# GpSimd's and ScalarE's part in the last block of a projection kernel: own weights, earlier copies, and partial dot products added in PSUM

## The chip, the cores and the metric

One core of a Trainium2 chip runs the whole program. The metric is the device time of one execution in microseconds; the kernel before took 636.08 us (median of 3 runs, 635.98 to 636.09).

Names used below: PE is the matrix engine (PEld its weight loads), DVE is VectorE, ACT is ScalarE, POOL is GpSimd, SP issues the loads. In the profile's lines CUSTOM_DVE_ANT_0 is DVE's dot product, TENSOR_TENSOR on POOL its product, ACTIVATE on ACT the sum of that product, and TENSOR_TENSOR_SCAN a scan. "A.", "V.", "G.", "T." and "SY." in code are ACT, DVE, POOL, PE and SP.

## The reference

```python
def setup_inputs():
    B, S, D = 8, 2048, 4096
    return {"x": randn(B, S, D), "w": randn(D, 1)}        # float32

def reference(x, w):
    proj = (x @ w).squeeze(-1)
    cm = np.maximum.accumulate(proj, axis=1)
    is_record = (proj >= cm).astype(np.float32)
    return np.cumsum(is_record, axis=1).astype(np.float32)
```

x has 268 MB, and every element is used once. The work is a dot product of length 4096 for each of 8 x 2048 positions, then a running maximum and a running count along 2048.

## The kernel before

Positions 0 to 1919 are handled in five groups of 384 (three rows of 4096 for each of 128 partitions), positions 1920 to 2047 in a tail of 128 (one row for each partition and batch row). Each dot product is split by columns. DVE multiplies and sums the first columns, with w in PSUM (`w_v`). POOL multiplies the others, with w in SBUF, and ACT sums POOL's products. PE brings the sums of all 128 partitions into 8 rows of PSUM by a matmul with the identity. DVE then runs three short instructions there: the maximum scan, the comparison, and the count scan.

```python
CM = 3072; CP = 2688; CL = 2304      # DVE's columns: in the groups, tiles 0-2, tiles 3-5
PIECES = {                           # the last two batch rows in pieces (start, split, end)
    1: [(1280, 3072, D), (0, 768, 1280)],
    0: [(2816, 3584, D), (1792, 2432, 2816), (1024, 1536, 1792),
        (512, 1024, 1024), (0, 512, 512)],
}
# ...
def scans(cm_, cnt_, n, cm0, cnt0):
    V.tensor_tensor_scan(out=cm_, data0=ps[:, :n], data1=neg[:, :n], ...)    # running max
    V.tensor_tensor(out=rec[:, :n], in0=ps[:, :n], in1=cm_, op=ALU.is_ge)
    V.tensor_tensor_scan(out=cnt_, data0=rec[:, :n], data1=rec[:, :n], initial=cnt0,
                         op0=ALU.add, op1=ALU.max)                           # running count
# ... ACT's loop over the groups ends with
            A.wait_ge(at, 1)         # DVE's queue raises at once it has gone past its scans
# ... the tail
A.copy(out=w_sb[:, CP:], in_=w_p)._wait_ge(fr[NS - 2], 2 * NK // NS).then_inc(wc, 1)
A.copy(out=w_sb[:, :CP], in_=w_v[:, :CP])._wait_ge(ge, NG).then_inc(wc, 1)
V.wait_ge(wc, 3)                     # both copies
G.wait_ge(wc, 2)                     # the first copy
for m, b in enumerate(last):         # six whole tiles, batch rows 7 to 2
    # ... DVE: columns below VC, PSUM w; POOL: the others, w_sb; ACT: sum of POOL's
for i, (b, (c0, v, c1)) in enumerate(tails):          # seven pieces, batch rows 1 and 0
    # ... DVE's dot is seeded with the sum of the piece before, so it waits for that one
lhs = [sum_p] + parts + [sum_v]      # POOL's sums of the pieces, then DVE's one sum
for k, l in enumerate(lhs):
    i = T.matmul(out=ps[:, :P], lhsT=l, rhs=identity, start=k == 0, ...)._wait_ge(*waits[k])
scans(cm_l, cnt_l, P, ...)
```

`w_sb` is a copy of all of w in an x buffer that has come free; `w_p` holds columns 2688 to 4095 of w in SBUF from the start. A copy is needed for POOL's other columns: the Trainium skill ("PSUM — Partial Sum Buffer", Specifications (TRN2)) has GpSimd neither read nor write PSUM.

## Time and profile before

| | before |
|---|---|
| time | 636.08 us |
| span in the profile | 634.0 us |
| mean load rate | 424 GB/s |
| last load lands | 623.44 us |
| last POOL product ends | 628.5 us |
| first short scan of the tail starts | 630.15 us |

Two rows of the profile's page, 40 equal slices of the span with busy tenths:

```profile
POOL 0444555544444444555444444555544444445496
DMA  9999999999999999999999999999999999999992
```

Loads fill the span until the last slice. POOL is at 4 or 5 tenths in the groups and still in slice 38, and full in slice 39. So only the end can be changed without moving fewer bytes.

When the last load landed is read from the issues of the last load's line (engine, operation, duration in ns, start; then time to landing). It was issued at 598.5 and landed 24.9 us later, at 623.44 with one more digit:

```profile
L191 SPq DMA_DIRECT2D xbuf<-in_x_dram x1: 4214/4214/4214, 598.5 to 598.5; - x1
DMA to landing us min/median/max: 24.9/24.9/24.9
```

The timeline of the end (start us, duration us, engine, line, operation, out<-in, shapes, count, and the idle time before with what ended it):

```profile
584.59 6.69 POOL L250 TENSOR_TENSOR xbuf<-xbuf,w_p 128x3072 f32<-128x3072 f32 x1 [7.81 <-POOLq L251]
...
598.98 1.01 DVE L139 TENSOR_TENSOR_SCAN cnt<-rec,cnt 8x384 f32<-8x384 f32 x1
599.26 1.36 ACT L285 COPY xbuf<-w_p 128x1408 f32<-128x1408 f32 x1 [4.72 <-ACTq L267]
600.53 2.39 ACT L286 COPY xbuf<-w_v 128x2688 f32<-128x2688 f32 x1
600.77 21.30 POOL L296 TENSOR_TENSOR xbuf<-xbuf 128x1408 f32<-128x1408 f32 x6 [9.49 <-ACT xbuf L285]
...
603.07 2.95 DVE L125 CUSTOM_DVE_ANT_0 xbuf<-xbuf,w_v 128x2688 f32<-128x2688 f32 x1 [3.09 <-ACT xbuf L286]
...
622.01 6.48 POOL L321 TENSOR_TENSOR xbuf<-xbuf 128x1024 f32<-128x1024 f32 x5
...
630.15 0.47 DVE L132 TENSOR_TENSOR_SCAN cm_l<-ps,cm,neg 8x128 f32<-8x128 f32 x1 [3.22 <-PE ps L336]
```

POOL's last group product ended at 584.59 + 6.69 = 591.28. POOL then stood idle for 9.49 us until ACT's first copy, although the first tail tile had landed at 589.20. ACT had been held back by its wait for DVE's scans (`at`). (DVE's queue raises such a signal when it has gone past the scans, not when they are done: ACT began 0.28 us after the count scan's start, and before its end at 599.99.) From 600.77 on POOL's eleven products run back to back for 27.7 us, and the chain of waits (start, duration, what) is nothing but them until ACT and PE finish:

```profile
599.26 1.37 ACT xbuf L285
...
603.89 18.19 POOL xbuf L296 x5
622.08 5.74 POOL xbuf L321 x4
...
628.51 1.61 PE ps L336 x6
```

### The profile page before, as it was taken

To read this page: it belongs to the slowest core of one execution; us is meant where nothing else is said; L and a number is where in the kernel's file an instruction comes from. 1 tells how busy PE (TensorE), PEld (TensorE's weight loads), DVE (VectorE), ACT (ScalarE), POOL (GpSimd) and SP (SyncE) were. 2 spreads that over 40 slices of the span, in tenths; PEclk is the share of its full clock that TensorE was granted. 3 is DMA by queue.
4 is the path that set the end of the run, shared out by engine and by line. 5 is a ranking of instruction groups with operands and counts; after the bars stand their busy time and mean duration, and the time that the engine had idled before them with its cause. 6 is when DMAs were issued, how large, how long until landed. Compare 5 with 4: busy or idle time off the path is not lost. (4 is left out here: it accounts for less than half of the span.)

```text
span 634.0 us, 1167 instructions
## 1 busy us (share of the span) xinstructions
PE 29.8 (5%) x84; PEld 13.1 (2%) x84; DVE 434.0 (68%) x286; ACT 149.0 (24%) x267; POOL 296.7 (47%) x59
## 2 busy tenths in 40 slices
PE   8000000010000001000000100000001000000101
PEld 3000000000000000000000000000000000000000
DVE  0666777787666678777776676777778766667695
ACT  1222222223222222222222222222222322222344
POOL 0444555544444444555444444555544444445496
DMA  9999999999999999999999999999999999999992
GB/s 389 409 443 440 440 409 443 441 432 422 443 437 432 425 443 437 431 425 440 440 423 434 437 443 416 440 437 441 419 440 434 443 412 447 435 444 407 431 424 110
DMA packets 7746, 268.54 MB, mean 424 GB/s; under 512 B 904, under 2 KB 952, under 8 KB 1728
## 3 DMA queue, kind: packets, MB, share of 16 engines
q1 hardware_dynamic: 7728, 268.50, 98.1%
q10 hardware_dynamic: 16, 0.02, 0.0%
q14 instruction: 2, 0.02, 0.0%
HBM read 268.45 MB, written 0.07 MB: 424 GB/s over the span
## 5 line engine op out<-in xcount | busy, mean ns | idle before, releaser
L125 DVE CUSTOM_DVE_ANT_0 xbuf<-xbuf,w_v 128x3072 f32<-128x3072 f32 (+3 forms) x128 | 415.1, 3293 | 176.6 <-DMA xbuf<-in_x_dram 173.6
L250 POOL TENSOR_TENSOR xbuf<-xbuf,w_p 128x3072 f32<-128x3072 f32 x40 | 267.7, 6693 | 321.5 <-POOLq L251 321.5
L257 ACT ACTIVATE xbuf<-xbuf 128x1024 f32<-128x1024 f32 x120 | 125.4, 1046 | 455.9 <-POOL xbuf L250 455.9
L273 PE MATMUL ps<-identity,small 128*8 128x128 f32 x60 | 13.6, 418 | 566.6 <-ACT xbuf L257 566.6
L296 POOL TENSOR_TENSOR xbuf<-xbuf 128x1408 f32<-128x1408 f32 (+1 forms) x6 | 21.3, 3598 | 9.5 <-ACT xbuf L285 9.5
L257 ACT ACTIVATION_READ_ACCUMULATOR xbuf<-xbuf 128x1 f32 x120 | 22.4, 187 | 0.0
L273 PEld LDWEIGHTS ps<-identity,small 128*8 128x8 f32 x60 | 7.3, 129 | 574.0 <-ACT xbuf L257 570.1
L132 DVE TENSOR_TENSOR_SCAN cm<-ps,cm,neg 8x384 f32<-8x384 f32 x5 | 5.0, 1004 | 15.3 <-PE ps L273 15.3
L145 PE MATMUL w_v<-w_row,identity 8*128 8x512 f32 x14 | 12.1, 1056 | 0.0
L300 ACT ACTIVATE xbuf<-xbuf 128x1408 f32<-128x1408 f32 (+1 forms) x6 | 9.2, 1537 | 11.2 <-POOL xbuf L296 11.2
L125 DVE DVE_READ_ACCUMULATOR2_ANT small<- 128x1 f32 x133 | 11.0, 82 | 0.0
L321 POOL TENSOR_TENSOR xbuf<-xbuf 128x512 f32<-128x512 f32 (+3 forms) x5 | 6.5, 1342 | 0.0
L139 DVE TENSOR_TENSOR_SCAN cnt<-rec,cnt 8x384 f32<-8x384 f32 x5 | 5.0, 1007 | 0.2
L145 PEld LDWEIGHTS w_v<-w_row,identity 8*128 8x128 f32 x14 | 4.6, 332 | 7.3 <-issue 7.3
L125 DVE CUSTOM_DVE_ANT_0 xbuf<-xbuf,w_v,small 128x512 f32<-128x512 f32 (+2 forms) x5 | 4.1, 827 | 0.7
L336 PE MATMUL ps<-identity,small 128*8 128x128 f32 x8 | 2.2, 406 | 30.6 <-ACT xbuf L326 30.6
L326 ACT ACTIVATE xbuf<-xbuf 128x512 f32<-128x512 f32 (+3 forms) x5 | 3.3, 651 | 1.4 <-POOL xbuf L321 1.3
L136 DVE TENSOR_TENSOR rec<-ps,cm 8x384 f32<-8x384 f32 x5 | 2.7, 546 | 0.2
L132 DVE TENSOR_TENSOR_SCAN cm_l<-ps,cm,neg 8x128 f32<-8x128 f32 x1 | 0.5, 471 | 3.2 <-PE ps L336 3.2
L285 ACT COPY xbuf<-w_p 128x1408 f32<-128x1408 f32 x1 | 1.4, 1365 | 4.7 <-ACTq L267 4.7
L286 ACT COPY xbuf<-w_v 128x2688 f32<-128x2688 f32 x1 | 2.4, 2392 | 0.0
L145 PE MATMUL ps<-w_row,identity 8*128 8x512 f32 x2 | 2.1, 1136 | 3.1 <-DMA w_row<-in_w_dram 3.1
(19 smaller groups left out, 8.9 us busy)
## 6 DMA issues: line engine op xcount, KB each, us to landing
xbuf<-in_x_dram SPq DMA_DIRECT2D x40, 6144.0 KB, 47.8
xbuf<-in_x_dram SPq DMA_DIRECT2D x6, 2048.0 KB, 42.7
xbuf<-in_x_dram SPq DMA_DIRECT2D x1, 1408.0 KB, 36.8
xbuf<-in_x_dram SPq DMA_DIRECT2D x2, 640.0 KB, 38.5
xbuf<-in_x_dram SPq DMA_DIRECT2D x1, 512.0 KB, 39.8
xbuf<-in_x_dram SPq DMA_DIRECT2D x2, 256.0 KB, 26.8
xbuf<-in_x_dram SPq DMA_DIRECT2D x1, 384.0 KB, 32.2
out_dram<-cnt SPq DMA_DIRECT2D x5, 12.0 KB
```

Source lines behind the costliest of these rows:

```text
L125: return V.tensor_tensor_reduce(out=xsl, in0=xsl, in1=wsl, scale=1.0, scalar=seed, op0=ALU.mult, op1=ALU.add, accum_out=dst,)
L132: V.tensor_tensor_scan(out=cm_, data0=ps[:, :n], data1=neg[:, :n], initial=cm0, op0=ALU.max, op1=ALU.max,)._wait_ge(psr, 1).then_inc(psr, 1)
L136: V.tensor_tensor(out=rec[:, :n], in0=ps[:, :n], in1=cm_, op=ALU.is_ge)._wait_ge(psr, 2).then_inc(psr, 1)
L139: V.tensor_tensor_scan(out=cnt_, data0=rec[:, :n], data1=rec[:, :n], initial=cnt0, op0=ALU.add, op1=ALU.max,)._wait_ge(psr, 3).then_inc(cs, 1)
L145: return T.matmul(out=w_v[:n, k * WC : (k + 1) * WC] if k < CV // WC else ps_w, lhsT=identity[:NW, k : k + 1].to_broadcast([NW, n]), rhs=w ...
L250: G.tensor_mul(out=xm, in0=xm, in1=w_m)._wait_ge(xg, 1).then_inc(pg, 1)
L257: i = A.activation(out=xr, in_=xr, func=ACTF.Copy, accum_out=sums_p[:, j * B + b : j * B + b + 1],)
L273: i = T.matmul(out=ps[:, j:NP:R], lhsT=l[:, j * B : (j + 1) * B], rhs=identity, start=l is sums_p, stop=l is sums,)
L296: G.tensor_mul(out=xb[:, VC:D], in0=xb[:, VC:D], in1=w_sb[:, VC:D])._wait_ge(xt[m], 16).then_inc(pl, 1)
L300: A.activation(out=xb[:, VC:D], in_=xb[:, VC:D], func=ACTF.Copy, accum_out=sum_p[:, b : b + 1],)._wait_ge(pl, npool)
L321: G.tensor_mul(out=xl, in0=xl, in1=w_sb[:, v:c1])._wait_ge(xq[i], 16).then_inc(pl, 1)
L326: A.activation(out=xl, in_=xl, func=ACTF.Copy, accum_out=pacc[:, b : b + 1])._wait_ge(pl, npool).then_inc(pa, 1)
```

## The change

The intent is to start the tail earlier and to take waits out of it. (1) POOL's first three tail tiles read `w_p`, which is there from the start. (2) ACT no longer waits for the last group's scans, and PE gives its signal `ge` once DVE's and ACT's sums are there, so both copies of w run beside PE and the scans. (3) In the tail every DVE dot product starts from zero instead of the sum before it (it is no longer "seeded"); PE adds all sums of a batch row in PSUM, nine of them instead of four. The trace shows two matmul records (passes) for each sum, called a pair below. 320 columns of the last pieces go from DVE to POOL.

```diff
-            (1024, 1536, 1792),
-            (512, 1024, 1024),
+            (1024, 1408, 1792),
+            (512, 832, 1024),
 ...
+        A.sem_inc(at, 1)
         with A.Fori(0, NG):
+            A.wait_ge(at, 1)
+            A.sem_inc(at, -1)
 ...
-            A.wait_ge(at, 1)
-            A.sem_inc(at, -1)
         with T.Fori(0, NG):
             T.wait_ge(ga, 1)
-            T.wait_ge(gd, 1)
-            for j in range(R):
-                for l in (sums_p, sums):
+            T.sem_inc(ga, -1)
+            for l in (sums_p, sums):
+                if l is sums:
+                    T.wait_ge(gd, 1)
+                    T.sem_inc(ge, 1)
+                for j in range(R):
                     i = T.matmul(
                         out=ps[:, j:NP:R], lhsT=l[:, j * B : (j + 1) * B],
-                        rhs=identity, start=l is sums_p, stop=l is sums,
+                        rhs=identity, start=l is sums_p and j == 0,
+                        stop=l is sums and j == R - 1,
                     )
 ...
-        V.wait_ge(wc, 3)
+        V.wait_ge(wc, 2)
 ...  # in the tail, one helper for whole tiles and pieces
+            dot(xb[:, c0:v], w_v[:, c0:v], sum_v[piece][:, b : b + 1])._wait_ge(arrived, 16)...
+            if v < c1:
+                wb = w_p[:, v - CP : c1 - CP] if npool < R else w_sb[:, v:c1]
+                if npool == R:
+                    G.wait_ge(wc, 2)
 ...  # PE's order: for each piece of batch row 0, DVE's sum and then POOL's
+                order.append((sum_v[piece], sd, len(last) + i + 1))
+                if v < c1:
+                    order.append((sum_p[piece], pa, npool))
```

With `start` now set on the first of six matmuls alone, the others find columns not yet written in this round. The Trainium skill ("PSUM — Partial Sum Buffer", The four PSUM rules) says that a starting matmul clears the written-marks of its whole 2 KiB bank (in the groups of 32 partitions that it writes), and that a later matmul overwrites where the mark is clear.

More of the change, by code (lines that the diff above doesn't have):

```diff
@@ L64 @@
     }
-    NPART = max(sum(v < c1 for _, v, c1 in p) for p in PIECES.values()) - 1
+    NPART = max(len(p) for p in PIECES.values())
     pool = ctx.enter_context(tc.tile_pool(name="sb", bufs=1))
@@ L98 @@
     sums_p = cut(R * B)
-    sum_v = cut(B)
-    sum_p = cut(B)
-    parts = [cut(B) for _ in range(NPART)]
     tails = [(b, p) for b in sorted(PIECES, reverse=True) for p in PIECES[b]]
-    acc = cut(len(tails))
+    sum_v = [cut(B) for _ in range(NPART)]
+    sum_p = [cut(B) for _ in range(NPART)]
     def row(k):
@@ L122, with dot @@
     V, A, G, T, SY = nc.vector, nc.scalar, nc.gpsimd, nc.tensor, nc.sync
-    def dot(xsl, wsl, seed, dst):
+    def dot(xsl, wsl, dst):
         return V.tensor_tensor_reduce(
-            out=xsl, in0=xsl, in1=wsl, scale=1.0, scalar=seed,
+            out=xsl, in0=xsl, in1=wsl, scale=1.0, scalar=0.0,
             op0=ALU.mult, op1=ALU.add, accum_out=dst,
@@ L231 @@
                     i = dot(
-                        row(slot * R + j)[:, :CM], w_v[:, :CM], 0.0,
+                        row(slot * R + j)[:, :CM], w_v[:, :CM],
                         sums[:, j * B + b : j * B + b + 1],
@@ L273 @@
                     i = T.matmul(
                         out=ps[:, j:NP:R], lhsT=l[:, j * B : (j + 1) * B],
-                        rhs=identity, start=l is sums_p, stop=l is sums,
+                        rhs=identity, start=l is sums_p and j == 0,
+                        stop=l is sums and j == R - 1,
                     )
             i.then_inc(psr, 1)
-            T.sem_inc(ga, -1)
             T.sem_inc(gd, -1)
-            T.sem_inc(ge, 1)
         w_sb = row(NS * R - 1 - R)
-        A.copy(out=w_sb[:, CP:], in_=w_p)._wait_ge(fr[NS - 2], 2 * NK // NS).then_inc(wc, 1)
+        A.copy(out=w_sb[:, CP:], in_=w_p)._wait_ge(fr[NS - 2], 2 * NK // NS)
@@ L286 @@
         A.copy(out=w_sb[:, :CP], in_=w_v[:, :CP])._wait_ge(ge, NG).then_inc(wc, 1)
-        V.wait_ge(wc, 3)
+        V.wait_ge(wc, 2)
         npool = 0
-        G.wait_ge(wc, 2)
-        for m, b in enumerate(last):
-            xb = row(m)
-            VC = CP if m < R else CL
-            if m == R:
-                G.wait_ge(wc, 3)
-            dot(xb[:, :VC], w_v[:, :VC], 0.0, sum_v[:, b : b + 1])._wait_ge(xt[m], 16)
-            G.tensor_mul(
-                out=xb[:, VC:D], in0=xb[:, VC:D], in1=w_sb[:, VC:D]
-            )._wait_ge(xt[m], 16).then_inc(pl, 1)
-            npool += 1
-            A.activation(
-                out=xb[:, VC:D], in_=xb[:, VC:D], func=ACTF.Copy,
-                accum_out=sum_p[:, b : b + 1],
-            )._wait_ge(pl, npool)
@@ L304 @@
-        nseed = 0
-        nact = 0
-        actn = []
-        for i, (b, (c0, v, c1)) in enumerate(tails):
-            xb = row(B - 1 - b)
-            if c1 == D:
-                seed, piece = 0.0, 0
-            else:
-                V.wait_ge(sd, nseed)
-            dst = acc[:, i : i + 1] if c0 else sum_v[:, b : b + 1]
-            dot(xb[:, c0:v], w_v[:, c0:v], seed, dst)._wait_ge(xq[i], 16).then_inc(
-                sd, 1
-            )
-            nseed += 1
-            seed = dst
-            if v < c1:
-                xl = xb[:, v:c1]
-                G.tensor_mul(out=xl, in0=xl, in1=w_sb[:, v:c1])._wait_ge(
-                    xq[i], 16
-                ).then_inc(pl, 1)
-                npool += 1
-                pacc = parts[piece - 1] if piece else sum_p
-                A.activation(
-                    out=xl, in_=xl, func=ACTF.Copy, accum_out=pacc[:, b : b + 1]
-                )._wait_ge(pl, npool).then_inc(pa, 1)
-                nact += 1
-                piece += 1
-                if b == 0:
-                    actn.append(nact)
@@ L333, with share @@
-        lhs = [sum_p] + parts + [sum_v]
-        waits = [(pa, n) for n in actn] + [(sd, nseed)]
-        for k, l in enumerate(lhs):
+        def share(xb, b, piece, c0, v, c1, arrived):
+            nonlocal npool
+            dot(xb[:, c0:v], w_v[:, c0:v], sum_v[piece][:, b : b + 1])._wait_ge(
+                arrived, 16
+            ).then_inc(sd, 1)
+            if v < c1:
+                wb = w_p[:, v - CP : c1 - CP] if npool < R else w_sb[:, v:c1]
+                if npool == R:
+                    G.wait_ge(wc, 2)
+                xl = xb[:, v:c1]
+                G.tensor_mul(out=xl, in0=xl, in1=wb)._wait_ge(arrived, 16).then_inc(
+                    pl, 1
+                )
+                npool += 1
+                A.activation(
+                    out=xl, in_=xl, func=ACTF.Copy,
+                    accum_out=sum_p[piece][:, b : b + 1],
+                )._wait_ge(pl, npool).then_inc(pa, 1)
@@ new lines @@
+        for m, b in enumerate(last):
+            share(row(m), b, 0, 0, CP if m < R else CL, D, xt[m])
+        order = []
+        for i, (b, (c0, v, c1)) in enumerate(tails):
+            piece = PIECES[b].index((c0, v, c1))
+            share(row(B - 1 - b), b, piece, c0, v, c1, xq[i])
+            if b == min(PIECES):
+                order.append((sum_v[piece], sd, len(last) + i + 1))
+                if v < c1:
+                    order.append((sum_p[piece], pa, npool))
+        for k, (l, s_, n) in enumerate(order):
@@ L336 @@
             i = T.matmul(
                 out=ps[:, :P], lhsT=l, rhs=identity,
-                start=k == 0, stop=k == len(lhs) - 1,
-            )._wait_ge(*waits[k])
+                start=k == 0, stop=k == len(order) - 1,
+            )._wait_ge(s_, n)
         i.then_inc(psr, 1)
```

## The prediction

> **What bounds the kernel now.** For most of the span it is the loads: the page's DMA row is at 9 tenths in every slice but the last (424 GB/s on average), and the waits view shows DVE waiting 173.6 us for loads. The change can only act on the end. The chain of waits starts at 599.26 us with ACT's copy of w (1.36 us), then runs through Pool almost without a gap: six tail products to 622.08, five small ones to about 628.5, then ACT's last sum, PE (1.6), three scans (1.3) and about 2.5 us to the end of the output write at 634.0. Yet the last load lands at 623.44 (issues with times to landing): the 10.6 us after it are catch-up. Pool had been idle since 591.28 (9.49 us, released by ACT's copy), although the first tail tile landed at 589.20 and the next two at 594.08 and 598.95. DVE also idled 3.09 us (599.99 to 603.07) for the second copy.
>
> **What the change does.**
> 1. Pool's first three tiles read w_p directly. Pool starts near 591.6 instead of 600.77.
> 2. ACT no longer waits for the last scans, and PE signals earlier: both copies (1.36 + 2.39 us) run at about 594.7 to 598.5, beside PE and scans. DVE can start its tail at about 600.1, 2.9 us earlier.
> 3. Unseeded dots remove DVE's 0.2 us gaps between small pieces; more PE matmuls, mostly hidden; 320 columns go from DVE to Pool (about 0.7 us at 2.17 ns a column).
>
> **Walked forward, with traced durations and landings.** Pool (3.13 us for 1408 columns, 3.96 for 1792) becomes limited by landings: the six big tiles begin at 591.6, 594.7, 599.0, 603.8, 608.7, 613.6. From there it runs without a gap: 617.56, then 1024, 512, 512, 384, 384, 192 columns (2.29, 1.24, 1.24, 0.95, 0.95, about 0.55) to 624.8. ACT's last sum ends near 625.4, PE's last two pairs (0.53 each, queued behind the third sum) near 626.5. DVE waits for landings from its seventh dot on; its last piece (landed 623.44) is done at 624.3. Then scans and write as before, 3.85 us: end at 630.4, 3.6 us less. Most of Pool's 9.2 us head start turns into waits for loads, since the loads' end does not move.
>
> **Predicted: 632.5 us, 631.6 to 633.6 in 8 of 10.** Faster by over 2% (under 623.4): 0.005, it would need an end before the last load lands. Within 2%: 0.985. Slower by over 2%: 0.01.
>
> **What would show each step.** Right: ACT's copies at 594.7 to 598.5; Pool's first tail product before 592.5, four later ones waiting 1 to 2 us for DMA; DVE's first tail dot at about 600.1; last landing 623.4 +/- 0.4; Pool ends near 624.8, DVE near 624.3; first short scan near 626.6; end minus last landing about 7 us. The five groups' PE and scan stretches stay as long as they are. Wrong: any of these missing, or last landing moved.
>
> **What could make it wrong.** The third Pool product would start about when the count scan does (598.98), which has both inputs in SBUF. The Trainium skill ("SBUF — State Buffer", Who interferes with whom) says such a DVE instruction contends with a GpSimd one that reads SBUF; this trace has no such overlap. If the scan waited for Pool, DVE would be 2 us late and the gain about 1 us smaller. Copies from PSUM beside the scans could be slower than alone. The loads' end could drift by some tenths.

## The result and the profile after

The kernel after took 632.88 us (median of 4 runs, 632.84 to 633.00), the kernel before 636.06 us beside it. Ratios are the mean time of one kernel's runs over that of the other's of the same rounds, so not quite the ratio of these medians: 0.995, 95% interval 0.9933 to 0.9968. The gain is 3.2 us, where 3.6 us was predicted.

| | before | after |
|---|---|---|
| span | 634.0 us | 630.8 us |
| last load lands | 623.44 us | 623.51 us |
| last POOL product ends | 628.49 us | 624.93 us |
| DVE's last dot product ends | 626.92 us | 625.01 us |
| first short scan of the tail starts | 630.15 us | 626.99 us |
| from last landing to that scan | 6.71 us | 3.48 us |

The last row is the best measure in what follows, because the end of the loads drifts by some tenths of a microsecond from run to run.

The two rows of the page; POOL's work has moved forward into slice 38:

```profile
POOL 0444555444444444555544444445554544444876
DMA  9999999999999999999999999999999999999994
```

The last load's issue and landing:

```profile
L189 SPq DMA_DIRECT2D xbuf<-in_x_dram x1: 4214/4214/4214, 598.6 to 598.6; - x1
DMA to landing us min/median/max: 25.0/25.0/25.0
```

The timeline of the end:

```profile
591.32 6.30 POOL L302 TENSOR_TENSOR xbuf<-xbuf,w_p 128x1408 f32<-128x1408 f32 x2
...
594.52 1.35 ACT L286 COPY xbuf<-w_p 128x1408 f32<-128x1408 f32 x1
...
595.78 2.39 ACT L287 COPY xbuf<-w_v 128x2688 f32<-128x2688 f32 x1
...
599.08 3.18 POOL L302 TENSOR_TENSOR xbuf<-xbuf,w_p 128x1408 f32<-128x1408 f32 x1 [1.46 <-DMA xbuf<-in_x_dram]
599.14 3.93 DVE L137 TENSOR_TENSOR_SCAN cnt<-rec,cnt 8x384 f32<-8x384 f32 x1
...
602.99 2.92 DVE L123 CUSTOM_DVE_ANT_0 xbuf<-xbuf,w_v 128x2688 f32<-128x2688 f32 x1
...
613.67 11.25 POOL L302 TENSOR_TENSOR xbuf<-xbuf 128x1792 f32<-128x1792 f32 x7 [0.89 <-DMA xbuf<-in_x_dram]
...
622.84 4.11 PE L322 MATMUL ps<-identity,small 128*8 128x128 f32 x18 [25.36 <-DVE small L123]
...
625.07 1.38 PEld L322 LDWEIGHTS ps<-identity,small 128*8 128x8 f32 x8 [0.43 <-ACT xbuf L306]
...
626.99 0.47 DVE L130 TENSOR_TENSOR_SCAN cm_l<-ps,cm,neg 8x128 f32<-8x128 f32 x1 [1.97 <-PE ps L322]
```

POOL now begins at 591.32, waits for its tiles instead of for w, and gets through its products 3.6 us earlier. ACT's copies run from 594.52 to 598.17. But the count scan, 1.01 us before, takes 3.93 us: POOL's third product began 60 ns ahead of it. DVE therefore starts its tail at 602.99, only 0.08 us earlier than before. On the chain of waits the stall stands as "issue" in front of DVE, and the chain goes through DVE to PE:

```profile
599.63 3.36 issue
602.99 2.92 DVE xbuf L123
...
622.84 4.13 PE ps L322 x18
```

Read alone, this chain says that the stalled scan costs about 3 us. The experiments ask whether it does.

### The profile page after: what moved, and what is told of

The parts are those of the page before. It is cut to its first block, busy times and chain, and to the rows that moved or that the text cites. A ratio compares the mean times of both kernels' runs of the same rounds, so it can differ in the third digit from the quotient of the medians.

```text
span 630.8 us, 1180 instructions
## 1 busy us (share of the span) xinstructions
PE 31.7 (5%) x94; PEld 14.2 (2%) x94; DVE 435.7 (69%) x286; ACT 149.2 (24%) x269; POOL 297.9 (47%) x60
## 5 line engine op out<-in xcount | busy, mean ns | idle before, releaser
L123 DVE CUSTOM_DVE_ANT_0 xbuf<-xbuf,w_v 128x3072 f32<-128x3072 f32 (+5 forms) x133 | 418.0, 3193 | 173.3 <-DMA xbuf<-in_x_dram 173.3
L275 PE MATMUL ps<-identity,small 128*8 128x128 f32 x60 | 13.6, 414 | 567.2 <-PEq L269 567.2
L258 ACT ACTIVATION_READ_ACCUMULATOR xbuf<-xbuf 128x1 f32 x120 | 22.4, 187 | 0.0
L302 POOL TENSOR_TENSOR xbuf<-xbuf 128x1792 f32<-128x1792 f32 (+4 forms) x9 | 19.2, 2162 | 3.4 <-DMA xbuf<-in_x_dram 3.4
L275 PEld LDWEIGHTS ps<-identity,small 128*8 128x8 f32 x60 | 7.3, 126 | 574.5 <-issue 570.6
L306 ACT ACTIVATE xbuf<-xbuf 128x1408 f32<-128x1408 f32 (+5 forms) x12 | 12.9, 1077 | 13.5 <-POOL xbuf L302 13.4
L302 POOL TENSOR_TENSOR xbuf<-xbuf,w_p 128x1408 f32<-128x1408 f32 x3 | 9.5, 3172 | 1.5 <-DMA xbuf<-in_x_dram 1.5
L137 DVE TENSOR_TENSOR_SCAN cnt<-rec,cnt 8x384 f32<-8x384 f32 x5 | 7.9, 1589 | 0.2
L322 PE MATMUL ps<-identity,small 128*8 128x128 f32 x18 | 4.1, 412 | 25.4 <-DVE small L123 25.4
L322 PEld LDWEIGHTS ps<-identity,small 128*8 128x8 f32 x18 | 1.7, 113 | 27.8 <-DVE small L123 26.1
L306 ACT ACTIVATION_READ_ACCUMULATOR xbuf<-xbuf 128x1 f32 x12 | 2.2, 187 | 0.0
```

The lines of the kernel that those rows point to most:

```text
L123: return V.tensor_tensor_reduce(out=xsl, in0=xsl, in1=wsl, scale=1.0, scalar=0.0, op0=ALU.mult, op1=ALU.add, accum_out=dst,)
L258: i = A.activation(out=xr, in_=xr, func=ACTF.Copy, accum_out=sums_p[:, j * B + b : j * B + b + 1],)
L275: i = T.matmul(out=ps[:, j:NP:R], lhsT=l[:, j * B : (j + 1) * B], rhs=identity, start=l is sums_p and j == 0, stop=l is sums and j == R - 1,)
L302: G.tensor_mul(out=xl, in0=xl, in1=wb)._wait_ge(arrived, 16).then_inc(pl, 1)
L306: A.activation(out=xl, in_=xl, func=ACTF.Copy, accum_out=sum_p[piece][:, b : b + 1],)._wait_ge(pl, npool).then_inc(pa, 1)
```

## The experiments

Two theories at first. A: the stall is slack. POOL's products from the landing at 613.61 on, ACT's third sum of the last batch row at 625.03, and PE's four queued pairs after it set the end. B: the chain is right, and DVE's lateness sets the end. "Gap" below is from the last landing to the tail's first short scan. Letters V0 to V4 are DVE's sums for the five pieces of batch row 0, P0 to P3 POOL's. PE's order in the kernel after is V0 P0 V1 P1 V2 P2 V3 P3 V4.

| run | what it is | time, us (range) | gap, us |
|---|---|---|---|
| before | | 636.06 (635.98-636.09) | 6.71 |
| after | all three parts | 632.88 (632.84-633.00) | 3.48 |
| b_own_w | part 1 alone | 633.67 (633.56-633.86) | 4.18 |
| b_act_early | part 2 alone | 633.50 (633.48-633.59) | 4.03 |
| b_all | parts 1 and 2 | 633.50 (633.43-633.68) | 3.98 |
| b_tail | part 3 alone | 637.81 (637.34-637.93) | 7.95 |
| a_no_own_w | parts 2 and 3 | 633.07 (632.93-633.81) | 3.74 |
| a_scan | after, scan not stalled | 632.86 (632.62-633.05) | 3.42 |
| a_pool_late | after, scan not stalled, another way | 633.47 (633.34-633.59) | 3.45 |
| a_order | after, PE's order changed | 632.71 (632.21-632.88) | 3.38 |
| a_scan_order2 | after, both | 632.08 (631.97-632.11) | 2.58 |
| best2 | that, with the old split | 631.76 (631.65-632.01) | 2.27 |
| b_all_scan | parts 1 and 2, scan not stalled | 631.81 (631.64-631.94) | 2.23 |

The kernel before was run beside each batch; its medians were 636.0 to 636.2 us. All runs gave correct results.

### Taking the stall away (a_scan)

```diff
         V.tensor_tensor(
-            out=rec[:, :n], in0=ps[:, :n], in1=cm_, op=ALU.is_ge
+            out=ps[:, :n], in0=ps[:, :n], in1=cm_, op=ALU.is_ge
 ...
-            out=cnt_, data0=rec[:, :n], data1=rec[:, :n], initial=cnt0,
+            out=cnt_, data0=ps[:, :n], data1=neg[:, :n], initial=cnt0,
```

The second operand only takes part in a maximum that it never wins, so the very negative constant does as well as the flags. The timing of everything else stays.

> The kernel after, but the record flags are written over the projections in PSUM, and the count scan reads them there and the constant tile in SBUF: one SBUF input instead of two. Both theories expect the last group's count scan to fall from 3.93 us to about 1.0 and DVE's first tail dot to move from 603.0 to about 600.2. Theory A (the end is set by Pool from the landing at 613.61 on, then ACT's third sum at 625.03 and PE's four queued pairs of sums; DVE's 3 us stall is slack): time stays 632.9 +/- 0.15. Theory B (as the chain of waits reads: the stalled scan makes DVE late, and PE's 18 passes start late at 622.84 because of DVE): at least 0.5 us faster, up to 1.8.

The scan beside POOL's product, DVE's first tail dot, and PE at the end, from the timeline:

```profile
599.21 3.17 POOL L302 TENSOR_TENSOR xbuf<-xbuf,w_p 128x1408 f32<-128x1408 f32 x1 [1.43 <-DMA xbuf<-in_x_dram]
599.30 1.00 DVE L137 TENSOR_TENSOR_SCAN cnt<-ps,cnt,neg 8x384 f32<-8x384 f32 x1
...
600.23 2.92 DVE L123 CUSTOM_DVE_ANT_0 xbuf<-xbuf,w_v 128x2688 f32<-128x2688 f32 x1
...
617.10 2.02 DVE L123 CUSTOM_DVE_ANT_0 xbuf<-xbuf,w_v 128x1792 f32<-128x1792 f32 x1 [0.77 <-DMA xbuf<-in_x_dram]
...
623.37 3.68 PE L322 MATMUL ps<-identity,small 128*8 128x128 f32 x16 [1.55 <-ACT xbuf L306]
...
625.17 1.38 PEld L322 LDWEIGHTS ps<-identity,small 128*8 128x8 f32 x8 [0.43 <-ACT xbuf L306]
```

The mechanism is confirmed: with one SBUF input the scan runs in 1.00 us beside the same POOL product. The Trainium skill ("SBUF — State Buffer", Who interferes with whom) says that a DVE instruction with two SBUF inputs contends with a GpSimd one that reads SBUF, and one with a single SBUF input does not. Both halves agree with 3.93 and 1.00 us. But the time did not move (632.86 against 632.88), as A had it. DVE gained 2.8 us and spent most of it waiting for loads, from its seventh dot on (617.10); its last dot ended at 624.38, 0.6 us earlier than in the kernel after. The PE line shows why nothing came of the rest: P0 comes from ACT and is second in PE's order, so eight pairs still stand behind 623.37, and they end at 627.05. (They wait once more, shortly, for P2 at 625.17, after which four pairs are left, as in the kernel after.)

### Who goes first (a_pool_late)

```diff
             V.sem_inc(at, 1)
+            V.sem_inc(sg, 1)
 ...
+                if npool == R - 1:
+                    G.wait_ge(sg, NG)
```

> The kernel after, with one added wait: Pool's third tail product (the one the count scan overlaps, started 60 ns before the scan) may begin only once DVE's sequencer has gone past the last group's scans, some 0.2 us after the count scan has begun. If the one that holds the shared reads first keeps them to its end: the scan takes 1.0 us, Pool's product waits for it (ends near 603.2 instead of 602.3, still before its next tile lands at 603.9), DVE starts its tail at 600.2. If Pool wins whatever the order: the scan again takes over 3 us and DVE starts after 602.5. If they share: both stretched in part. The time stays 632.9 +/- 0.2 in every case, as with the scan mended in the other way, because the order on PE is not touched.

The scan and POOL's third product:

```profile
599.16 1.01 DVE L137 TENSOR_TENSOR_SCAN cnt<-rec,cnt 8x384 f32<-8x384 f32 x1
...
599.44 3.71 POOL L305 TENSOR_TENSOR xbuf<-xbuf,w_p 128x1408 f32<-128x1408 f32 x1 [1.80 <-DVEq L242]
```

With two SBUF inputs again, but 0.28 us ahead of POOL, the scan takes 1.01 us and POOL's product is 0.5 us longer than 3.18. POOL begins before the scan's end because the signal is raised as DVE's queue goes past the scan, as with `at` above. So whichever of the two begins first holds up the other. In both orders the later one ended 0.2 us sooner than its own length after the first one's end (the scan at 603.07 in the kernel after, where POOL's 602.26 and 1.01 make 603.27; POOL here at 603.15, where the scan's 600.17 and 3.18 make 603.35). The gap (3.45 us) and the span (630.8 us) equal those of the kernel after, a second sign that the stall itself is slack there. The measured time, however, was 633.47 us, outside the expected 632.9 +/- 0.2: 0.6 us more than the kernel after, of which its profiled execution shows nothing within the span. Most of it lies outside the span: time less span is 2.4 to 2.6 us in all four executions here, and 2.0 to 2.2 in every execution of most kernels. What it is stays open. The added semaphore isn't needed for it: three of the four executions of b_tail and two of the four of a_no_own_w, which have no new semaphore, show 2.4 to 2.6 us too.

### PE's order alone (a_order)

```diff
+        order = [order[k] for k in (0, 1, 2, 3, 4, 6, 5, 8, 7)]   # V0 P0 V1 P1 V2 V3 P2 V4 P3
         for k, (l, s_, n) in enumerate(order):
```

> The kernel after, with PE's order of the nine pairs changed alone: DVE's fourth sum (done at 624.41) goes ahead of Pool's third (done at 625.03), and DVE's last ahead of Pool's last. Theory A: three pairs instead of four are left after 625.03, one pair is 0.47 us, so about 632.4. Theory B (DVE's lateness and the sheer number of passes): unchanged, 632.9.

```profile
622.67 4.01 PE L323 MATMUL ps<-identity,small 128*8 128x128 f32 x18 [25.34 <-DVE small L123]
...
623.94 2.25 PEld L323 LDWEIGHTS ps<-identity,small 128*8 128x8 f32 x12 [0.31 <-ACT xbuf L306]
```

These are PE's lines of its timeline. 632.71 us against 632.88, and a gap of 3.38 against 3.48: 0.1 to 0.2 us of the expected 0.47. Theory A falls as a full account. The loads of weights show no wait in the last twelve passes: PE is now busy with a backlog from 623.94 on, and V3, which went ahead, took the time that P2's wait had left idle. A pair takes 4.01 / 9 = 0.45 us, so nine pairs from V0 (622.67, when late DVE delivers it) end at 626.7 whatever their order. (This profile has the lower granted clock, 0.62, but the pairs are no slower: in an unbroken queue they start 0.43 us apart here and in the kernel after.)

### Both together (a_scan_order2)

This led to theory C: PE's queue sets the end. It is held by DVE's late V0 and by P0's place in the order, and either is enough.

```diff
 # the scan as in a_scan, and
+        order = [order[k] for k in (0, 2, 4, 1, 6, 3, 8, 5, 7)]   # V0 V1 V2 P0 V3 P1 V4 P2 P3
```

> The kernel after with both obstacles of PE's queue taken away at once: the count scan with one SBUF input (so DVE's sums are ready 0.6 to 1.7 us earlier), and PE's order by readiness: DVE's first three sums, Pool's first, DVE's fourth, Pool's second, DVE's fifth, Pool's third and fourth. New theory C: PE's queue of nine pairs at 0.46 us each sets the end; with the scan alone it runs without slack from Pool's first sum (623.3, eight pairs left), with the order alone from DVE's first sum (622.7, nine pairs left), so neither alone helps, and both together leave six pairs after 623.3: end of PE near 626.2 instead of 627.0, 632.05 +/- 0.2. If the two edits are as worthless together as apart: 632.8.

```profile
622.28 3.85 PE L323 MATMUL ps<-identity,small 128*8 128x128 f32 x16 [0.54 <-DVE small L123]
...
626.17 0.47 DVE L130 TENSOR_TENSOR_SCAN cm_l<-ps,cm,neg 8x128 f32<-8x128 f32 x1 [1.86 <-PE ps L323]
```

632.08 us against 632.05 expected: 0.8 us faster than the kernel after, where the scan's edit alone gave 0.02 and a_order's change of order 0.17. (This order is another one, and was not run beside the stalled scan. An estimate from the trace of the kernel after: nine pairs from V0 at 622.84, 0.43 us apart, end at about 626.9 in any order, against 626.95 there.) PE has eight pairs to do from 622.28, where in a_scan it had eight from 623.37. So the stalled scan does cost time, but only once PE's order lets the earlier sums through. The new order moves P0 back and P2 too, and which of the two moves counts was not tested apart. An estimate from a_scan's trace says P0: eight pairs without a break from 623.37, 0.43 us apart, would end at 627.0, so P2's place alone was worth 0.1 us at most there.

### Each part of the change alone

Part 1 alone (b_own_w):

```diff
-        G.wait_ge(wc, 2)
 ...
-                out=xb[:, VC:D], in0=xb[:, VC:D], in1=w_sb[:, VC:D]
+                out=xb[:, VC:D], in0=xb[:, VC:D], in1=w_p if m < R else w_sb[:, VC:D]
```

> The kernel before with one part of the change: Pool's first three tail tiles use w_p and do not wait for the copies. Pool then meets its landings, but DVE still starts at about 603.1 (second copy) and is in charge at the end: its last small dot ends near 626.9 as before, PE's last pair near 627.5 against 630.1: about 633.4 (2.6 us faster than before). If DVE's start near 603 did not matter in that kernel, it would go to about 631.6.

Part 2 alone (b_act_early) takes the changes of ACT's and PE's loops as in the diff of the change, and one wait more, because PE's first tail matmul was ordered after the scans only by ACT's old wait:

```diff
+        T.wait_ge(cs, NG)
         for k, l in enumerate(lhs):
```

> The kernel before with the second part of the change alone: ACT does not wait for the last scans and PE signals earlier [...]. Pool still waits for ACT's first copy, so starts near 596.1 instead of 600.8. Expected: Pool has caught up before the tile landed at 613.6, exactly as with its own w; the count scan is stalled by the Pool product it overlaps (about 4 us), DVE's first tail dot stays near 603.1, so the same end as with Pool's own w alone: 633.6 +/- 0.25. If the scan is not stalled here, DVE starts at 600.2 and the time is about 631.6.

Parts 1 and 2 (b_all) are these two edits in one kernel:

> The change without its third part: Pool's own w and ACT early, but the seeded dots, the old split and five pairs of sums on PE. The count scan is stalled as in the kernel after, so DVE starts at about 603.0, ends its seeded dots near 626.8, and PE has one pair left: 633.5 +/- 0.2, the same as with either part alone (633.67 and 633.50). The third part is then worth about 0.65 us in the kernel after, where it cost 1.6 us in the kernel before. If the first two parts add up: 631 or less.

The scan and PE's last pair in b_all's timeline:

```profile
599.04 3.91 DVE L139 TENSOR_TENSOR_SCAN cnt<-rec,cnt 8x384 f32<-8x384 f32 x1
...
626.75 0.60 PE L339 MATMUL ps<-identity,small 128*8 128x128 f32 x2 [1.58 <-DVE small L125]
```

633.67, 633.50 and 633.50 us: either part gives 2.5 to 2.7 us, and together they give no more. (The expectation of b_all miscounts PE's pairs: the seeded tail has four, not five; b_all_scan's below has the same slip.) The two replace each other. Each lets POOL catch up before (part 1) or nearly at (part 2) the landing near 613.6, and in each DVE still starts at 603, so its last seeded dot and one pair of PE end it, as the last line shows (PE waited 1.58 us for DVE). What keeps DVE there is the stalled scan; in b_own_w ACT's second copy would do it as well (it ends at 602.98, the scan at 603.03). The scan took 3.99, 3.97 and 3.91 us in these three runs. In b_own_w its record even begins 20 ns before POOL's, so the start of a record isn't quite the moment at which the reads are taken:

```profile
599.04 3.99 DVE L139 TENSOR_TENSOR_SCAN cnt<-rec,cnt 8x384 f32<-8x384 f32 x1
599.06 3.16 POOL L295 TENSOR_TENSOR xbuf<-xbuf,w_p 128x1408 f32<-128x1408 f32 x1 [1.48 <-DMA xbuf<-in_x_dram]
```

The kernel after with part 1 taken out (a_no_own_w):

```diff
-                wb = w_p[:, v - CP : c1 - CP] if npool < R else w_sb[:, v:c1]
+                wb = w_sb[:, v:c1]          # and POOL waits for the first copy
```

> The kernel after, but Pool's first three tail tiles use the copied w as before, so Pool waits for ACT's first copy (done about 595.9) and starts near 596 instead of 591.3. Theory A: Pool catches up before the tile landed at 613.61, so nothing is lost: 632.9 +/- 0.15. If Pool's early start were what pays: 1 us or more slower. Whether the count scan is stalled here depends on who starts first near 599.1; under A it does not show in the time.

633.07 us, 0.2 us slower than the kernel after, just outside the expected band. POOL starts at 596.14 instead of 591.32, so of its 4.8 us only a few tenths were needed: the sixth tile starts at 614.07, 0.35 us after its landing at 613.72.

Part 3 alone (b_tail) is the kernel before with the new tail, POOL waiting for the first copy as before:

> The kernel before with the third part of the change alone: unseeded dots, nine pairs of sums on PE, 320 columns more on Pool; Pool and ACT start as before. Expected slower: Pool ends about 0.8 us later (0.27 for 128 columns more and 0.55 for a new product of 192), and four queued pairs of 0.47 us instead of two follow ACT's third sum: about 1.2 us, 637.3 +/- 0.4. If the part were free or a gain by itself: 636.2 or less.

```profile
600.99 28.53 POOL L300 TENSOR_TENSOR xbuf<-xbuf 128x1408 f32<-128x1408 f32 x12 [9.49 <-ACT xbuf L283]
...
629.67 1.38 PEld L320 LDWEIGHTS ps<-identity,small 128*8 128x8 f32 x8 [0.42 <-ACT xbuf L304]
```

637.81 us (0.1 us above the expected band), 1.6 us slower than before: twelve products instead of eleven keep POOL until 629.52, and four pairs (eight loads of weights) follow ACT's third sum. Of the 1.6 us only 1.2 are of this kind (a gap of 7.95 against 6.71, as expected); the other 0.4 lie outside the span, as in a_pool_late. Part 3 by itself is a loss where POOL is in charge. On top of parts 1 and 2 it is a gain of 0.6 us (633.50 to 632.88), because there DVE, late by the stall, is in charge.

### Mending what part 3 pays for (b_all_scan, best2)

b_all_scan is b_all with the scan's edit of a_scan:

> The kernel before with the first two parts of the change (Pool's own w, ACT early), without the third (seeded dots, five pairs, old split stay), and the count scan with one SBUF input. Theory C: DVE starts at 600.2, meets its landings, seeds cost little because DVE waits for landings anyway; its last dot ends near 625.2, PE has one pair left after it: PE ends near 625.8 instead of 627.0, about 631.6 +/- 0.3, faster than the kernel after though it lacks the third part. If unseeding is needed for the gain: 632.8 or more.

best2 is a_scan_order2 with the old split of columns and the order V0 V1 V2 P0 V3 P1 V4 P2:

> The kernel after with the count scan with one SBUF input, the split of columns of the kernel before (320 columns back on DVE, one Pool product fewer, eight pairs) and PE's order by readiness. Theory C: from Pool's first sum at 623.3 on PE has five and a half pairs left, its end moves to about 625.8: 631.7 +/- 0.2, about what the seeded version with the scan mended took (631.81). If the 192-column product and the ninth pair cost nothing: 632.1, as with the order alone.

631.81 and 631.76 us. Both beat both kernels: 4.2 to 4.4 us under the kernel before of the same batch, 1.1 us under the kernel after. b_all_scan has no part 3 at all. It differs from b_all in the scan's edit alone, and that edit was worth 1.7 us there (633.50 to 631.81), where it was worth 0.02 us in the kernel after. PE's end and the short scan after it in b_all_scan's timeline:

```profile
624.10 1.60 PE L339 MATMUL ps<-identity,small 128*8 128x128 f32 x6 [0.26 <-ACT xbuf L328]
...
625.75 0.47 DVE L132 TENSOR_TENSOR_SCAN cm_l<-ps,cm,neg 8x128 f32<-8x128 f32 x1 [0.82 <-PE ps L339]
```

So once the scan is not stalled, unseeding brings no more time: the seeds delay the end of DVE's last dot by 0.7 us (1.40 us after the last landing, against 0.71 in best2, which has the same split of columns), but PE then has only four pairs to do.

## Why the prediction was right

The predicted time (632.5, range 631.6 to 633.6) holds the measured 632.88, and the gain was right to 0.4 us in 3.6.

- **Right: what bounds the kernel.** The loads did not move (last landing 623.44 and 623.51). Everything happened after 591 us.
- **Right: POOL.** It was predicted to start near 591.6 and end at 624.8; measured 591.32 and 624.93. Four of its products waited for loads, 0.88 to 1.67 us each (1 to 2 predicted). ACT's last sum was predicted near 625.4, and its record ends at 625.42.
- **Right: ACT's copies.** 594.7 to 598.5 predicted, 594.52 to 598.17 measured, at their old durations beside the scans.
- **Wrong: "DVE can start its tail at about 600.1".** It started at 602.99. It never waited for a load in the tail, where this was predicted from its seventh dot on, and its last dot ended at 625.01 instead of 624.3. What happened was the risk named in the prediction's last part: the count scan waited for POOL's third product. The cost put on it there ("the gain about 1 us smaller") was wrong too: a_scan and a_pool_late show that the stall by itself cost the kernel after no more than 0.1 us of gap. That the number survived the stall is luck: the prediction gave no reason why it should. PE's queue happened to be held up by something else as well (a_scan_order2), while without part 3 the same stall costs 1.7 us (b_all and b_all_scan).
- **Wrong term of the sum: "PE's last two pairs (0.53 each, queued behind the third sum)".** The last two pairs (P3 and V4) did take 1.06 us, but they did not begin when ACT's last sum was there (625.42). P2, released at 625.07, and V3 stood before them in the queue, so they began at 625.89, 0.47 us later. This is the 0.4 us (short scan near 626.6 predicted, 626.99 measured). That PE is a queue which two separate things hold up was not seen at all; a_order and a_scan_order2 showed it.
- **Partly wrong: part 3 as a small gain.** It was put down as removed DVE gaps with "more PE matmuls, mostly hidden". Alone they are not hidden: b_tail's gap grew by 1.2 us. The part gains 0.6 us only as an answer to DVE's lateness.
- **Not said: that parts 1 and 2 replace each other.** The prediction noted that most of POOL's 9.2 us head start turns into waits for loads. The runs show that the two parts alone bring 2.5 and 2.7 us, and 2.5 us together (each against the kernel before of its batch).

The last two pairs, P3 and V4, in PE's timeline of the kernel after (`--engine PE --window 626.11:627`):

```profile
625.89 1.06 PE L322 MATMUL ps<-identity,small 128*8 128x128 f32 x4
```

## What to carry to other kernels

Once loads set the time of most of a kernel, only the distance from the last landing to the end can be shortened. Measure that distance: it is free of the loads' drift. When two engines are moved to overlap for the first time, look for an instruction that suddenly takes longer (here 1.01 to 3.93 us), and check whether one of its two SBUF inputs can be read from PSUM instead. And before crediting a stall with its full length, take it away: here the same stall was worth 1.7 us without part 3, and nothing in the kernel after until the order of PE's queue was changed as well, because two causes held up the same queue.

## What the Trainium skill lacked or had wrong

- "SBUF — State Buffer", Who interferes with whom: it states the contention of a two-input DVE instruction with GpSimd's reads, which the runs confirm. The page also says (SBUF: two separate sides) that the one that starts first has the shared ports for its whole instruction. It gives no measured case of a scan. Here the count scan took 3.91 to 3.99 us instead of 1.01 beside POOL's 3.2 us product, and POOL's product took 3.71 us instead of 3.18 when the scan had begun 0.28 us before it; the one held up ended 0.2 us sooner than a wait for the whole of the other would give.
- The same section says that the order of issue decides who blocks. No run contradicts it, but in one (b_own_w) the scan's record began 20 ns before POOL's and it was the scan that was held (3.99 us): within some tens of ns the profile's starts do not tell who wins.
- None of the pages that I read gives the time of adding one more [128 x 8] float32 sum by a matmul with the identity. In these traces it is two matmul records, 0.60 us alone (b_all's last pair), and each further sum in an unbroken queue starts 0.43 us after the one before (1.06 us for the last two of the kernel after).
- No page that I read covers the time outside the span, which here is 2.0 to 2.2 us in most executions and 2.4 to 2.6 us in nine (all four of a_pool_late, three of b_tail, two of a_no_own_w); the cause is open.
